# Stick-breaking logits from 64 array rows a head, in place of zero-padded queries of 128 rows

## The chip, the core and the metric

The kernel runs on one core of a Trainium2 chip. Its engines work side by side, each through its own queue in a fixed order: PE (TensorE) multiplies matrices into the eight PSUM banks, DVE (VectorE) and ACT (ScalarE) do elementwise work and read PSUM, POOL (GpSimd) does elementwise work on SBUF alone, SP (SyncE) starts most DMA transfers. Each waits only where its next instruction needs what another has not finished. The metric is the device time of one execution in microseconds (us), the median over runs.

## What is computed

One layer with 512 tokens and 16 meta tokens ahead of them, width 1024: two mixers side by side, an output projection with layer norm, and a mixture of 16 experts. The change concerns the second mixer, "stick breaking", with 8 heads of 64 columns:

```python
def stick_breaking_mixer(q, k, v, norm_g):
    qh = heads(q) * (SB_DH ** -0.5)
    kh, vh = heads(k), heads(v)
    for blk in range(Lp // Q_BLOCK):
        start = blk * Q_BLOCK
        end = start + Q_BLOCK
        z = jnp.einsum('bhqd,bhkd->bhqk', qh[:, :, start:end], kh[:, :, :end])
        mask = jnp.arange(end)[None, :] < (start + jnp.arange(Q_BLOCK))[:, None]
        log_keep = jnp.where(mask, jax.nn.log_sigmoid(-z), 0.0)
        log_a = jax.nn.log_sigmoid(z) + lax.cumsum(log_keep, axis=3, reverse=True) - log_keep
        a = jnp.where(mask, jnp.exp(log_a), 0.0)
        outs.append(jnp.einsum('bhqk,bhkd->bhqd', a, vh[:, :, :end]))
```

After both mixers, `layer_norm(ALPHA * h + mixed @ w_out)` is routed, and each token goes to two of the 16 experts.

## The kernel before

**Stages.** Until 243.5 us of the profiled execution PE makes the input projections (`projections`, L333), seven groups of 512 columns, each in three fp32r products of high and low parts (`mm3`, L126 to L130); the heads of the first mixer are woven in between. The last group is the stick-breaking queries. From 243.5 to about 365 us `stick_breaking` (L568) and `out_proj` (L815) are woven (L907). Then tokens are routed, and from about 392 us on the 16 experts run: their weights are split into a high part (ACT, L900) and a low part (DVE, L901) and multiplied.

**Queries and keys.** The projected keys of a pair of heads lie in one tile `skT[pr]` of 128 rows, 64 for each head. `ev_sq` (L386) evacuates a group's four products, each with the queries of one pair, into eight tiles `sqZ`: head 2c has its queries in rows 0 to 63 and zeros in the others, head 2c+1 the reverse. The zeros are POOL memsets (L393), the upper halves go through ACT (L395), the lower through DVE (L397). Two buffers of the pool `big` hold the eight tiles. A product of `sqZ[h]` with `skT[pr]` then runs over all 128 rows, of which 64 add nothing.

**A head.** `sb_weights` (L484) makes one head's logits in PSUM banks `pj` (there are four): for the last query block (528 keys) two banks of 264 columns, for the others one bank. A bf16 product with an identity (L493, L499) adds the mask. Then Abs (ACT, L504), a maximum with zero (DVE L508, for every fourth head ACT L506), Exp and Ln (ACT, L509, L510), a scan along the keys (DVE, L513), a subtraction of the scan from the logits (DVE, L515), which is the last reader of the bank, and a final Exp (ACT, L516). `sb_values` (L521) transposes the weights of a pair of heads (PE L529, copied by DVE L531) and multiplies them with the values (PE L536), one pair behind. `sb_finish` (L539) closes a block of queries. `UNITS` (L479) gives the order: the last query block with four pairs, then the third, then the first two together.

**The output projection.** `out_proj` first takes buffers of the pool `big` for two broadcast rows (loaded by ACT's queue, L236), for two raw weight tiles (`wo_half`, SP's queue, L716) and for their high and low parts (ACT L725, DVE or POOL L124 and L122). Per block of 128 tokens it runs 24 instructions of `mm3` into two `z` banks, and DVE adds the result to the residual (L832). The first half of the weights serves four blocks, the second half (L722, L723) comes later: 192 instructions in all.

**What sets the order.** A build step lists each engine's queue from the program's order, the dependences and when buffers of a pool come free; it is fixed before the run. The pool `big` has 14 buffers, and the pool `free` (L850) of seven takes the memory of `upool`, which is closed at L849 when the first mixer is done. The first seven expert loads go there (`pump`, L871), and each load waits until the third before it has landed (`DEPTH`).

Of the kernel before, what the change touches and what calls it, by code (L numbers as in the profile page):

```python
# [13 lines left out]
AF = mybir.ActivationFunctionType  # L14
OP = mybir.AluOpType
# [3 lines left out]
P = 128  # L19
# [62 lines left out]
def hymba_kernel(ctx: ExitStack, tc: tile.TileContext, x, meta, w_in, lbnd, hgg, sbg, w_out, ln1g, ln1b,  # L82
                 wrg, brg, wre, bre, wg, wu, wd, ln2g, ln2b, out):
    nc = tc.nc
    V = nc.vector
# [18 lines left out]
    pj = lambda shape=None: bank("pj", 4, shape)  # L104
# [86 lines left out]
    for i2 in range(2):  # L191
        xr_ = xr[i2]
        for i1 in range(2):
            i = 2 * i2 + i1
# [25 lines left out]
    for m in (16, 8, 4, 2, 1):  # L220
        t = upool.tile([P, P], I32, tag=f"lm{m}", bufs=1, name=f"lm{m}")
# [9 lines left out]
    identb = att.tile([P, P], BF, name="identb")  # L231
    maskb = att.tile([P, P], BF, name="maskb")
# [136 lines left out]
            yield 1  # L369


    skT, sqZ, svt = [], [], []
    vbd = att.tile([P, 512], F32, name="vbd")

    def ev_sk(c, acc):
# [8 lines left out]
            V.tensor_copy(skT[c][:, 0:NM], p_[:, c, :])  # L384

    def ev_sq(c, acc):  # L386
        if c % 2 == 0:
            t = big_tile(4)
            sqZ.extend(t[:, j] for j in range(4))
        for s in range(2):  # L390
            q_ = sqZ[2 * c + s]
            r, o = slice(64 * s, 64 * s + 64), slice(64 * (1 - s), 64 * (1 - s) + 64)
            nc.gpsimd.memset(q_[o], 0.0)  # L393
            if s:
                nc.scalar.activation(q_[r], acc[r], AF.Copy, scale=0.125)  # L395
            else:
                V.tensor_scalar(q_[r], acc[r], 0.125, None, op0=OP.mult)  # L397

    def ev_sv(i, acc):
        if i == 0:  # L400
# [80 lines left out]

    relu = [0]

    def sb_weights(pr, s, am, qts, spans, n):  # L484
        h = 2 * pr + s
        pieces = []
        if n == 528:
            for a in range(2):
                z = pj()
                nc.tensor.matmul(z[:, 0:264], sqZ[h][:, 384:512], skT[pr][:, 264 * a:264 * a + 264],  # L490
                                 start=True, stop=not a)
                pieces.append((z, 264 * a, 264))
            nc.tensor.matmul(z[:, 136:264], identb, maskb, start=False, stop=True)  # L493
        else:
            z = pj()
            for i, (a, b) in zip(qts, spans):
                nc.tensor.matmul(z[:, a:b], sqZ[h][:, i * P:(i + 1) * P], skT[pr][:, 0:b - a],
                                 start=True, stop=False)
                nc.tensor.matmul(z[:, b - P:b], identb, maskb, start=False, stop=True)  # L499
            pieces.append((z, 0, n))  # L500
        ll, cc = tt(), tt("zs", ZS_BUFS)
        relu[0] += RELU_SHARE
        for z, a, w in pieces:
            nc.scalar.activation(ll[:, a:a + w], z[:, 0:w], AF.Abs)  # L504
            if relu[0] // 8 != (relu[0] - RELU_SHARE) // 8:
                nc.scalar.activation(cc[:, a:a + w], z[:, 0:w], AF.Relu)  # L506
            else:
                V.tensor_scalar(cc[:, a:a + w], z[:, 0:w], 0.0, None, op0=OP.max)  # L508
        nc.scalar.activation(ll[:, 0:n], ll[:, 0:n], AF.Exp, scale=-1.0)  # L509
        nc.scalar.activation(ll[:, 0:n], ll[:, 0:n], AF.Ln, bias=1.0)  # L510
        for a, b in spans:
            rv = slice(b - 1, a - 1 if a else None, -1)
            V.tensor_tensor_scan(cc[:, rv], cc[:, rv], ll[:, rv], 0.0, op0=OP.add, op1=OP.add)  # L513
        for z, a, w in pieces:
            V.tensor_sub(cc[:, a:a + w], z[:, 0:w], cc[:, a:a + w])  # L515
        nc.scalar.activation(cc[:, 0:n], cc[:, 0:n], AF.Exp)  # L516
        for m, (a, b) in enumerate(spans):
            (nc.gpsimd if n != 416 else V).tensor_copy(am[:, m, h * NM:(h + 1) * NM], cc[:, a:a + NM])
        return cc
# [48 lines left out]
    def stick_breaking():  # L568
        todo = []
        st = {}  # L570

        def drain():
            pr, qts, spans, prs, am, bank_, zz = todo.pop(0)
            if pr == prs[0]:
                st["o"] = bank_()
            sb_values(prs.index(pr), pr, prs, st["o"], zz, qts, spans)
            if pr == prs[-1]:
                sb_finish(am, st["o"], prs, qts)

        for qts, spans, n, groups in UNITS:  # L580
            for g, prs in enumerate(groups):
                am = att.tile([P, 2, P], F32, tag="am", bufs=3, name="am")
                if len(prs) < 4:
                    nc.gpsimd.memset(am, 0.0)
                for m, pr in enumerate(prs):
                    zz = []
                    for s in range(2):
                        zz.append(sb_weights(pr, s, am, qts, spans, n))
                        yield 1
                    todo.append((pr, qts, spans, prs, am, pj if g == 1 else otb, zz))  # L590
                    if len(todo) > 1:
                        drain()
                        yield 1
        for i, bank_ in ((0, zb), (1, pj)):
            acc2[i] = [bank_(), bank_()]
            for n_ in range(EARLY):
                wo_mm(i, 4, wo2, acc2[i], (n_,))
        drain()
# [586 lines left out]
    for hf in range(2):  # L1185
# [9 lines left out]
        for k in range(4):  # L1195
            c = 4 * hf + k
# [223 lines left out]
```

## Time and profile before

| what | us |
|---|---|
| median of three runs (729.41 to 730.34) | 730.28 |
| profiled execution | 727.62 |
| its span, first to last instruction | 725.9 |
| PE busy in the span | 658.3 (91%) |
| DVE busy | 550.8 (76%) |
| ACT busy | 426.0 (59%) |
| POOL busy | 189.3 (26%) |
| heads of the last query block | 243.5 to 272 |
| heads of the other query blocks, output projection | 272 to 365 |
| experts | 392.5 to the end |

The busy times are sums over the span, and their shares are averages over stages with different limits. A matmul's row shows its latency, so consecutive rows overlap: how long PE needs for one is read from the distance of two starts.

### The profile page before, as it was taken

The page shows a single profiled execution, that of the slowest core. Times are in us where ns is not written, and L with a number is a line of the kernel's source. Part 1 is how long each engine was busy: PE and PEld are TensorE (multiplying, and loading weights), DVE is VectorE, ACT ScalarE, POOL GpSimd, SP SyncE. Part 2 cuts the span into 40 slices and gives each one's busy share as a digit, 9 for nine tenths or more (in the row PEclk, how much of TensorE's full clock was granted, in tenths as well). Part 3 has the DMA queues.
Part 4 walks back from the last instruction along what each step waited for, and adds up shares of the span by engine and source line. Part 5 has one row for each costly group of instructions (what it writes and reads, how often), then busy time and mean ns, then how long its engine had stood idle before and what let it go on. Part 6 is the DMA issues. An engine that isn't in the chain of part 4 may idle for free. (4 is left out here: it accounts for less than half of the span.)

```text
span 725.9 us, 9414 instructions
## 1 busy us (share of the span) xinstructions
PE 658.3 (91%) x3366; PEld 530.3 (73%) x3366; DVE 550.8 (76%) x851; ACT 426.0 (59%) x640; POOL 189.3 (26%) x187
## 2 busy tenths in 40 slices
PE   6999999999999999988775799999999999999870
PEld 5878878777877777777665688888778788787650
DVE  5333064655564896999678999999999999999885
ACT  5353243535262674946214588768688686798682
POOL 5101144333243100112352023413114132112213
PEclk9999999999999999999997899999999999999995
DMA  9341111030004870303552899999999999998612
GB/s 348 121 120 58 59 59 58 4 113 1 1 1 163 304 287 0 117 1 119 224 216 99 290 339 339 351 326 368 329 348 377 335 362 334 334 360 280 216 41 114
DMA packets 62307, 143.67 MB, mean 198 GB/s; under 512 B 7370, under 2 KB 7402, under 8 KB 62256
## 3 DMA queue, kind: packets, MB, share of 16 engines
q1 hardware_dynamic: 53600, 128.98, 49.2%
q0 software_dynamic: 5904, 12.82, 6.0%
q10 hardware_dynamic: 2752, 1.22, 0.8%
q8 instruction: 28, 0.46, 0.2%
q14 instruction: 23, 0.19, 0.1%
HBM read 137.01 MB, written 14.68 MB: 209 GB/s over the span
## 5 line engine op out<-in xcount | busy, mean ns | idle before, releaser
L901 DVE TENSOR_TENSOR b<-b 128x1024 fp32r<-128x1024 f32 x192 | 225.2, 1221 | 4.6 <-ACT b L900 4.6
L900 ACT ACTIVATE b<-b 128x1024 fp32r<-128x1024 f32 x192 | 189.5, 1054 | 14.9 <-PE pj L130 12.3
L128 PE MATMUL pj<-b 128*128 128x512 f32 x264 | 108.1, 412 | 3.4 <-ACTq L1088 2.6
L129 PE MATMUL pj<-b 128*128 128x512 f32 x264 | 106.5, 404 | 0.6 <-DVE b L124 0.6
L130 PE MATMUL pj<-b 128*128 128x512 f32 x264 | 106.3, 403 | 0.0
L129 PE MATMUL pj<-b,xl 128*128 128x512 f32 x224 | 87.7, 391 | 2.7 <-DVE xl L1200 2.7
L128 PE MATMUL pj<-b,xh 128*128 128x512 f32 x224 | 89.3, 400 | 0.2 <-ACT b L900 0.2
L130 PE MATMUL pj<-b,xh 128*128 128x512 f32 x224 | 86.3, 401 | 0.5 <-DVE b L901 0.5
L963 POOL DMA_INDIRECT xg<-h1d,idx x15 | 21.9, 1460 | 175.4 <-DVE gate L960 73.0
L128 PEld LDWEIGHTS pj<-b 128*128 128x128 f32 x264 | 50.6, 192 | 14.5 <-ACTq L1088 2.7
L124 DVE TENSOR_TENSOR b<-b 128x1024 fp32r<-128x1024 f32 x24 | 33.1, 1391 | 35.4 <-ACT b L329 31.9
L130 PEld LDWEIGHTS pj<-b 128*128 128x128 f32 x264 | 51.0, 193 | 11.2 <-issue 0.5
L129 PEld LDWEIGHTS pj<-b 128*128 128x128 f32 x264 | 51.1, 194 | 10.9 <-DVE b L124 0.9
L1010 POOL DMA_INDIRECT ad<-y,idx x14 | 46.7, 3334 | 39.8 <-ACT b L900 27.6
L129 PEld LDWEIGHTS pj<-b,xl 128*128 128x128 f32 x224 | 42.1, 188 | 11.6 <-DVE xl L1200 3.1
L130 PEld LDWEIGHTS pj<-b,xh 128*128 128x128 f32 x224 | 42.0, 188 | 11.2 <-DVE b L901 2.6
L329 ACT ACTIVATE b<-b 128x1024 fp32r<-128x1024 f32 x28 | 29.3, 1056 | 35.4 <-PE pj L130 15.2
L128 PEld LDWEIGHTS pj<-b,xh 128*128 128x128 f32 x224 | 42.1, 188 | 9.0 <-ACT b L900 1.5
L626 ACT ACTIVATE zs<-zs 128x512 f32<-128x512 f32 x28 | 17.7, 632 | 48.1 <-POOL zs L625 48.0
L122 POOL TENSOR_TENSOR b<-b 128x1024 fp32r<-128x1024 f32 x8 | 19.6, 2446 | 92.5 <-ACT b L329 73.0
L624 POOL TENSOR_TENSOR zs<-u 128x256 f32<-128x256 f32 x28 | 22.2, 793 | 63.7 <-issue 25.9
L513 DVE TENSOR_TENSOR_SCAN zs<-zs,t 128x528 f32<-128x528 f32 (+3 forms) x32 | 32.8, 1046 | 2.0 <-ACT t L510 1.9
(339 smaller groups left out, 1325.3 us busy)
## 6 DMA issues: line engine op xcount, KB each, us to landing
b<-in_w_exp_gate_dram SPq DMA_DIRECT2D x32, 1024.0 KB, 8.3
b<-in_w_exp_up_dram SPq DMA_DIRECT2D x32, 1024.0 KB, 8.3
b<-in_w_exp_down_dram SPq DMA_DIRECT2D x32, 1024.0 KB, 10.0
b<-in_w_in_dram SPq DMA_DIRECT2D x12, 1024.0 KB, 5.0
b<-in_x_dram SPq DMA_DIRECT2D x8, 512.0 KB, 8.0
b<-in_w_out_dram SPq DMA_DIRECT2D x4, 1024.0 KB
b<-in_w_in_dram SPq DMA_DIRECT2D x4, 512.0 KB
h1d<-b POOLq DMA_DIRECT2D x4, 512.0 KB, 2.9
```

Source lines behind the costliest of these rows:

```text
L122: nc.gpsimd.tensor_sub(dst, src, hi)
L124: V.tensor_sub(dst, src, hi)
L128: nc.tensor.matmul(acc, ah, bh, start=first, stop=False)
L129: nc.tensor.matmul(acc, al, bh, start=False, stop=False)
L130: nc.tensor.matmul(acc, ah, bl, start=False, stop=last)
L329: latest[0] = nc.scalar.activation(wt[:, 0], src, AF.Copy).ins
L513: V.tensor_tensor_scan(cc[:, rv], cc[:, rv], ll[:, rv], 0.0, op0=OP.add, op1=OP.add)
L624: nc.gpsimd.tensor_sub(xv[:, :, 0, :], ref, bv[:, :, 0, :])
L900: nc.scalar.activation(t[:, 0], raw, AF.Copy)
L901: V.tensor_sub(t[:, 1], raw, f32(t[:, 0]))
L963: nc.gpsimd.indirect_dma_start(out=dst, out_offset=None, in_=h1d, in_offset=bass.IndirectOffsetOnAxis(ap=idx, axis=0), bounds_check=T - 1, ...
L1010: nc.gpsimd.indirect_dma_start(out=ad, out_offset=bass.IndirectOffsetOnAxis(ap=idx, axis=0), in_=y, in_offset=None, bounds_check=T - 1, oo ...
```

## The change

`ev_sq` writes one tile `sqT[c]` of 128 rows a pair, as the keys have it, with one ACT instruction; the memsets and the DVE half are gone, and one buffer of `big` is used where there were two. A new function `sb_logits` makes the products of both heads of a pair: operands are rows 0 to 63 for the first head and 64 to 127 for the second, one behind the other, and the masks of both follow. `sb_weights` gets the finished banks.

```diff
     def ev_sq(c, acc):
-        if c % 2 == 0:
+        if c == 0:
             t = big_tile(4)
-            sqZ.extend(t[:, j] for j in range(4))
-        for s in range(2):
-            q_ = sqZ[2 * c + s]
-            r, o = slice(64 * s, 64 * s + 64), slice(64 * (1 - s), 64 * (1 - s) + 64)
-            nc.gpsimd.memset(q_[o], 0.0)
-            if s:
-                nc.scalar.activation(q_[r], acc[r], AF.Copy, scale=0.125)
-            else:
-                V.tensor_scalar(q_[r], acc[r], 0.125, None, op0=OP.mult)
+            sqT.extend(t[:, j] for j in range(4))
+        nc.scalar.activation(sqT[c], acc, AF.Copy, scale=0.125)
...
-    def sb_weights(pr, s, am, qts, spans, n):
-        h = 2 * pr + s
-        pieces = []
+    def sb_logits(pr, qts, spans, n):
+
+        pieces = [], []
+        rows = [slice(64 * s, 64 * s + 64) for s in range(2)]
         if n == 528:
             for a in range(2):
-                z = pj()
-                nc.tensor.matmul(z[:, 0:264], sqZ[h][:, 384:512], skT[pr][:, 264 * a:264 * a + 264],
-                                 start=True, stop=not a)
-                pieces.append((z, 264 * a, 264))
-            nc.tensor.matmul(z[:, 136:264], identb, maskb, start=False, stop=True)
+                z = [pj(), pj()]
+                for s, r in enumerate(rows):
+                    nc.tensor.matmul(z[s][:, 0:264], sqT[pr][r, 384:512], skT[pr][r, 264 * a:264 * a + 264],
+                                     start=True, stop=not a)
+                    pieces[s].append((z[s], 264 * a, 264))
+            for s in range(2):
+                nc.tensor.matmul(z[s][:, 136:264], identb, maskb, start=False, stop=True)
         else:
-            z = pj()
+            z = [pj(), pj()]
             for i, (a, b) in zip(qts, spans):
-                nc.tensor.matmul(z[:, a:b], sqZ[h][:, i * P:(i + 1) * P], skT[pr][:, 0:b - a],
-                                 start=True, stop=False)
-                nc.tensor.matmul(z[:, b - P:b], identb, maskb, start=False, stop=True)
-            pieces.append((z, 0, n))
+                for s, r in enumerate(rows):
+                    nc.tensor.matmul(z[s][:, a:b], sqT[pr][r, i * P:(i + 1) * P], skT[pr][r, 0:b - a],
+                                     start=True, stop=False)
+                for s in range(2):
+                    nc.tensor.matmul(z[s][:, b - P:b], identb, maskb, start=False, stop=True)
+            for s in range(2):
+                pieces[s].append((z[s], 0, n))
+        return pieces
+
+    def sb_weights(pr, s, pieces, am, qts, spans, n):
+        h = 2 * pr + s
...
+                    pieces = sb_logits(pr, qts, spans, n)
                     for s in range(2):
-                        zz.append(sb_weights(pr, s, am, qts, spans, n))
+                        zz.append(sb_weights(pr, s, pieces[s], am, qts, spans, n))
```

The queues change in more places than the diff. SP's queue after the last loads for the input projections, before (`in_w_out` are the output projection's weights, `in_w_exp` the experts'):

```order
L179 DMA b<-in_w_in_dram 128x4x512 x12
L716 DMA b<-in_w_out_dram 128x2x1024 x2
L877 DMA b<-in_w_exp_gate_dram 128x4x512
L877 DMA b<-in_w_exp_up_dram 128x4x512
L877 DMA b<-in_w_exp_gate_dram 128x4x512
```

and in the changed kernel:

```order
L881 DMA b<-in_w_exp_gate_dram 128x4x512
L881 DMA b<-in_w_exp_up_dram 128x4x512
L881 DMA b<-in_w_exp_gate_dram 128x4x512
L720 DMA b<-in_w_out_dram 128x2x1024 x2
L828 DMA b<-in_x_dram 128x1024 x4
```

The two weight loads of the output projection have moved behind all seven of the first expert loads (the last three of them are shown).

ACT's queue from the end of the first mixer to the first heads, before (`b<-b 128x1024` at L725 are the splits of the output projection's weights, `b<-pj` the queries' evacuation, `t<-pj` the Abs):

```order
L469 ACTIVATE t<-oT 128x512
L725 ACTIVATE b<-b 128x1024
L472 ACTIVATE t<-z,eps_rms 128x512
L725 ACTIVATE b<-b 128x1024
L473 ACTIVATE t<-t 128x512
L463 ACTIVATE b<-t 128x512
L725 ACTIVATE b<-b 128x1024 x2
L395 ACTIVATE b<-pj 64x512 x2
L504 ACTIVATE t<-pj 128x264
L395 ACTIVATE b<-pj 64x512 x2
```

and in the changed kernel, where the same splits (now L729) stand, at the third and fourth pair of the last query block:

```order
L729 ACTIVATE b<-b 128x1024 x2
L519 ACTIVATE zs<-zs 128x528
L507 ACTIVATE t<-pj 128x264 x2
L512 ACTIVATE t<-t 128x528
L509 ACTIVATE zs<-pj 128x264
L513 ACTIVATE t<-t 128x528
L507 ACTIVATE t<-pj 128x264
L509 ACTIVATE zs<-pj 128x264
L512 ACTIVATE t<-t 128x528
L513 ACTIVATE t<-t 128x528
L729 ACTIVATE b<-b 128x1024 x2
L519 ACTIVATE zs<-zs 128x528 x2
```

The splits stood before the first head and now stand inside the work of the last pairs.

PE's queue at the second pair of the last query block, before (`tr<-ident,zs` are the transposes of the first pair's weights, `z<-b` the output projection):

```order
L490 MATMUL pj<-skT,b 128x264 x2
L493 LDWEIGHTS identb
L493 MATMUL pj<-maskb,identb 128x128
L529 MATMUL tr<-ident,zs 128x128 x4
L490 MATMUL pj<-skT,b 128x264 x2
L493 LDWEIGHTS identb
L493 MATMUL pj<-maskb,identb 128x128
L129 MATMUL z<-b 128x512
```

and in the changed kernel:

```order
L485 MATMUL pj<-skT,b 128x264 x2
L532 MATMUL tr<-ident,zs 128x128 x4
L485 MATMUL pj<-skT,b 128x264 x2
L489 LDWEIGHTS identb
L489 MATMUL pj<-maskb,identb 128x128
L489 LDWEIGHTS identb
L489 MATMUL pj<-maskb,identb 128x128
L532 MATMUL tr<-ident,zs 128x128 x4
L539 MATMUL oT<-b,aT 128x64 x8
```

The first two products were both halves of one head's keys; now they are the first half of both heads, and the second halves of both come after the transposes. No output-projection instruction stands between. PE's queue now has none of them until the fourth pair's products, where before it had 25 up to there.

## Rows read from the trace of the kernel before

**Rows 1.** Stretch, busy us of PE, PEld, DVE, ACT, POOL (instructions); clock, DMA share, GB/s.
```profile
243.50:272.00 28.50, 26.63 (x151) 20.94 (x150) 25.41 (x46) 21.49 (x47) 2.08 (x8) 1.00 0.85 331
272.00:288.50 16.50, 16.06 (x84) 11.87 (x83) 9.96 (x17) 6.02 (x13) 1.17 (x5) 1.00 0.00 0
288.50:307.00 18.50, 18.03 (x102) 13.81 (x101) 16.76 (x26) 16.95 (x33) 3.22 (x6) 1.00 0.35 115
...
392.50:726.00 333.50, 299.15 (x1413) 237.86 (x1412) 308.18 (x404) 246.10 (x304) 79.79 (x36) 0.96 0.85 297
```
**Rows 2.** Timeline of PE (start us, us, engine, line): products of queries and keys, mask.
```profile
250.04 1.16 PE L490 MATMUL pj<-skT,b 128*128 128x264 f32 x4 [0.26 <-DVE zs L515]
251.03 0.22 PE L493 MATMUL pj<-maskb,identb 128*128 128x128 bf16 x1
...
288.25 0.84 PE L497 MATMUL pj<-skT,b 128*128 128x400 f32 x2
288.92 0.22 PE L499 MATMUL pj<-maskb,identb 128*128 128x128 bf16 x1
```
**Rows 3.** Timeline of PE around a 16-row product, then two full ones.
```profile
228.38 0.39 PE L130 MATMUL pj<-b 128*128 128x512 f32 x1
228.70 0.48 PE L674 MATMUL tr<-u,t 16*128 16x128 f32 x2
229.11 0.94 PE L676 MATMUL tr<-b,t 128*128 128x128 f32 x6
...
231.02 0.39 PE L686 MATMUL oT<-qd,t 128*128 128x128 f32 x2
231.25 0.39 PE L685 MATMUL oT<-aT,b 128*128 128x128 f32 x2
```
**Rows 4.** Timeline of ACT and DVE around the queries' evacuation; in brackets idle before.
```profile
233.40 1.06 ACT L725 ACTIVATE b<-b 128x1024 fp32r<-128x1024 f32 x1 [0.40 <-DMA b<-in_w_out_dram]
...
240.28 1.23 DVE L124 TENSOR_TENSOR b<-b 128x1024 fp32r<-128x1024 f32 x1 [0.26 <-ACT b L725]
241.74 2.72 DVE L397 TENSOR_SCALAR b<-pj 64x512 f32<-64x512 f32 x4 [0.23 <-PE pj L130]
...
245.09 1.08 ACT L395 ACTIVATE b<-pj 64x512 f32<-64x512 f32 x2
```
**Rows 5.** Groups of ACT, 240 to 306: count | busy us, mean ns | idle before.
```profile
L504 ACT ACTIVATE t<-pj 128x264 f32<-128x264 f32 x16 | 5.9, 384 | 1.0 <-PE pj L490 0.9
L509 ACT ACTIVATE t<-t 128x528 f32<-128x528 f32 x8 | 5.2, 649 | 0.1
```
**Rows 6.** Timeline of DVE: first scan; second, fourth and eighth head's subtractions.
```profile
248.26 1.26 DVE L513 TENSOR_TENSOR_SCAN zs<-zs,t 128x528 f32<-128x528 f32 x1
...
251.52 0.77 DVE L515 TENSOR_TENSOR zs<-pj,zs 128x264 f32<-128x264 f32 x2
...
258.42 0.76 DVE L515 TENSOR_TENSOR zs<-pj,zs 128x264 f32<-128x264 f32 x2
...
271.15 0.77 DVE L515 TENSOR_TENSOR zs<-pj,zs 128x264 f32<-128x264 f32 x2
```
**Rows 7.** Timeline of POOL, the first three of eight memsets.
```profile
215.36 1.64 POOL L393 MEMSET b<- 64x512 f32 x3
```
**Rows 8.** Timeline of SP's DMA queue: start us, us, line, issue.
```profile
228.58 3.90 SPq L716 DMA_DIRECT2D b<-in_w_out_dram  x2
238.77 0.37 SPq L877 DMA_DIRECT2D b<-in_w_exp_gate_dram  x1
...
249.42 0.37 SPq L877 DMA_DIRECT2D b<-in_w_exp_up_dram  x1
252.03 0.37 SPq L877 DMA_DIRECT2D b<-in_w_exp_gate_dram  x1
```
**Rows 9.** Timeline of PE after waits, at the lower clock.
```profile
355.27 0.63 PE L129 MATMUL pj<-b 128*128 128x512 f32 x1
355.70 0.63 PE L130 MATMUL pj<-b 128*128 128x512 f32 x1
```

More of the change, by code (lines that the diff above doesn't have):

```diff
@@ L369, in projections @@
             yield 1
-    skT, sqZ, svt = [], [], []
+    skT, sqT, svt = [], [], []
     vbd = att.tile([P, 512], F32, name="vbd")
```

## Prediction

> **What bounds the kernel now.** I read the page's totals first, then the busy times by stretch, then the timeline of each queue from 215 to 310 us. The profiled execution takes 727.62 us, of which the span is 725.9; the median of the three runs is 730.28, so 2.66 us more. PE is busy 91% of the span, as the table above has it, but that is an average over stages. From 392.5 us on the experts run, and PE (299.15) and DVE (308.18) fill the 333.5 us between them [rows 1]. The change touches nothing there, and the stage starts when routing is known, so whatever the attention stage gains or loses before it should reach the end one for one. What decides is 243.5 to 365 us, where the stick-breaking heads and the output projection share the engines. With the eight heads of the last query block (243.5 to 272) DVE is busy 25.41 of 28.5 us. Then, from 272 to 288.5, PE is full (16.06 of 16.5) while DVE has only 9.96 us of work: PE catches up with the output projection. From 288.5 to 307 both are nearly full. So DVE with its chain through ACT sets the first stretch, and PE the second.
>
> **The products themselves.** A head's product against keys has two instructions for each 264 columns. Two such products and the mask's turn take 250.04 to 251.03, so about 0.5 us a product, and one of 400 columns takes 288.25 to 288.92, 0.67 us [rows 2]. Sixteen of the first, eight of the second and eight pairs of 144 and 272 columns (an estimate of 0.7 each, by columns) make 19 us. The operand now has 64 rows, but the columns streamed are as many, so PE gains only where the two heads of a pair run beside each other. No row of this trace shows two 64-row products, so the bounds are: nothing saved, or half, 9.5 us. The nearest row for other row counts is the 16-row product: the instruction before it starts at 228.38, it starts at 228.70 and the next full one at 229.11. Two such instructions took 0.50 us of PE's time where two full ones take 0.22 to 0.23 [rows 3], so a visit to another shape costs about 0.28 us. There are 20 visits in the new order (7 in the first query block, 5 in the second, 8 in the last): up to 5.6 us lost. I take neither end: half of the products' gain on 64 rows given back by visits, and no net saving on the path. [...]
>
> **The evacuation of the queries.** Before, DVE does four halves (241.74 to 244.46) and ACT four, the last ending at 246.17 [rows 4]. After, ACT does four full tiles at about 0.57 us, each as its product ends, so until 244.4. Then its order is three Abs of 0.38 (pipelined, 0.3 apart), an Exp of 0.65, an Abs and an Ln [rows 5], and the first scan can start at about 247.2 instead of 248.26 [rows 6]: 1.1 us gained. But ACT's new order puts the final Exp of the pair's first head ahead of the Ln of the second head. That Exp waits for scan and subtractions (1.26 and 0.7) until 249.1, Exp and Ln take it to 250.4, and with the second scan, one maximum and the subtractions [rows 6] the pair ends at 252.8, where before its last subtractions ran from 251.52 to 252.3. The gain is spent: +0.5 us.
>
> **Two heads at once in four banks.** With 528 columns a pair fills all four pj banks. Before, the next head's two banks were free as soon as one head's subtractions were done. Now the second halves of both heads of the next pair need the banks of both heads before. So after a pair's last subtraction there is a chain that DVE fills only in part: two products and masks (until about +0.7 us), two Abs, Exp, maximum on ACT, Ln (to +3.1), scan, subtractions, scan, subtractions (3.9): 7.0 to 7.1 us a pair without overlap, 6.6 with it. Before, the subtractions starting at 258.42 and 271.15 lie two pairs apart [rows 6], 6.4 us a pair. Pairs two and three cost +0.6 each: the third ends at about 266.9, +1.6 us in all.
>
> **The weights that come late.** This is what the change moves without saying so. The eight POOL memsets of 0.5 us from 215.36 on [rows 7] had no input, so, as I read the order, they claimed the query tiles' buffers early, and the output-projection weights, next in line for buffers of the same pool, could be loaded at 228.58 [rows 8] and split on ACT from 233.40 [rows 4]. Now the first writer of the query tile is ACT's evacuation at 241.7. In the new order the two weight loads stand behind seven expert loads on SP's queue. Those start at 238.77, are each held until the third before has landed, and by 249.42 and 252.03 advance 2.6 us a piece [rows 8]; four are still to land at 252. The broadcast rows that ACT loads now share the time. So the first weights land at about 262 to 265, the second 2.6 us later, and the 25 output-projection instructions that PE did ahead of the fourth pair cannot run there. Nothing else fills PE's gaps. ACT reaches the first two splits at about 267, so it hardly waits for the data, but the splits, 1.05 us each, now lie in its chain: two ahead of the third pair's last Exp and the fourth pair's Abs, two ahead of the fourth pair's final Exps. Three of the low parts (1.23 us each [rows 4]) lie in DVE's chain, one of them between the last scan and its subtractions. The fourth pair's first scan is then due at 271.9, its last subtraction ends at about 277.7; before, it ended at 271.9: **+5.8 us**. Then PE takes over: its queue up to the next pair holds 70 output-projection instructions less the first 12, at 0.23 us, the transposes and values between, and the second pair of the next query block starts its product at about 295.0, before at 288.25 [rows 2]: **+6.8**. Up to that point 76 of the 192 output-projection instructions were done before, 70 are now, so no more is left over than 6 times 0.23 us.
>
> **What is given back.** From 288.5 to 307 PE was nearly full, and the six heads that are left there have products of 4 us: up to 2 us saved with overlap, nothing without. DVE's idle 1.7 us there bounds the recovery. I take 0.8 us. The memsets that go and the 2.7 us of DVE that go were hidden: POOL and DVE both waited around them, with PE full ahead of 243.5. **Sum: 6.8 less 0.8, +6.0 us**, so 733.6 for an execution like the profiled one and 736.3 for the median. Bounds: with full overlap the three chains give back 0.45 each, the block's pair 0.67 and the block after some 1.2 more, +3; without overlap and with the price of each visit on the path (7 before 277, 5 in the next block, 3.4 us) and PE falling to its lower clock after a wait of some 5 us, as the 0.43 us from 355.27 to 355.70 shows (0.23 otherwise) [rows 9], +11.
>
> **Rivals.** (1) *The pairs do not run beside each other and the shape changes cost*: the change then does not do what it says, and gives the upper bound. For it speaks the 16-row product [rows 3], against it that a 64-row pair may lie in two halves of the array at once. [...] Time: 730.3 + 10, about 740. (2) *Faster*: PE is the bound of 272 to 307, and a pair side by side saves there 8 times 0.33 us, 2.7 us, while the first scan starts 1.1 us earlier. This decides if the late weights cost nothing, that is if they land by about 258, before the third pair's end, and their splits find ACT idle (it was busy 21.49 of 28.5 us [rows 1]). Time: about 727.5. Against it: seven loads at 2.6 us stand in front. (3) *No change*: the 25 instructions moved (5.8 us) are paid by 64-row pairs (4 us up to 288.5) and by the gaps that PE has later, since from 307 on DVE sets the pace: 730 to 731.5. Against it: DVE was idle 6.5 us from 272 to 288.5 because PE was late, and will be again.
>
> **How the numbers follow.** Forecast 62% (733.5 to 738.5), rival 1 17%, rival 2 10%, rival 3 11%. The time is the forecast's, 736.3. The range leaves out the faster rival, half of the no-change one and the far end of rival 1: 730.5 to 742. Within 0.2% is 728.8 to 731.7, about what measurement can tell from no change. Faster 0.10, same 0.11, slower 0.79.
>
> **What will show it.** The weight loads issued after about 250 us on SP instead of 228.58; ACT's first split after 262; no output-projection product before the fourth pair; the last subtraction of the 528-column heads near 277; PE full between there and the next block's second pair at about 295; the expert stage as long as before, 333.5 us. Starts of the two products of a pair within some 0.1 us of each other would show overlap; 0.25 apart per instruction, none. Wrong would be: weights landed before 258, subtractions two pairs apart still 12.8 us, or an expert stage that shortens.

## The result, and the profile after

The changed kernel takes 740.45 us (median of 4 runs, 738.66 to 741.25), the kernel before beside it 729.85: a ratio of 1.0141, 95% interval [1.0112, 1.0170], so 10.6 us slower. The forecast was 736.3, with a range of 730.5 to 742. The direction and the range hold, the size was too small, and the time that came is almost the one that rival 1 gave, for a cause that was not rival 1's. The profiled execution took 741.25 us, with a span of 739.5.

The page's totals and clock row (40 slices, tenths of full speed):

```profile
span 739.5 us, 9413 instructions
PE 666.1 (90%) x3366; PEld 533.2 (72%) x3366; DVE 548.9 (74%) x847; ACT 424.6 (57%) x640; POOL 176.4 (24%) x179
...
PEclk9999999999999669999997999999999999999895
```

The same stretches as in [rows 1], from the first product of queries and keys on (columns as there):

```profile
243.40:278.70 35.30, 30.62 (x136) 23.11 (x136) 27.40 (x45) 23.79 (x49) 3.98 (x7) 0.66 0.87 334
278.70:297.00 18.30, 17.17 (x89) 13.04 (x87) 10.05 (x18) 5.39 (x12) 2.80 (x7) 1.00 0.01 1
297.00:403.80 106.80, 85.67 (x539) 68.88 (x538) 89.10 (x195) 48.07 (x103) 28.89 (x25) 0.92 0.35 129
403.80:739.50 335.70, 300.37 (x1412) 238.92 (x1412) 307.86 (x403) 245.92 (x304) 71.16 (x36) 0.95 0.85 295
```

The heads of the last query block take 35.3 us instead of 28.5, and PE's granted clock in them is 0.66 instead of 1.00. SP's queue shows why (start, us, line, issue):

```profile
249.21 0.37 SPq L881 DMA_DIRECT2D b<-in_w_exp_up_dram  x1
253.26 0.37 SPq L881 DMA_DIRECT2D b<-in_w_exp_gate_dram  x1
253.68 1.01 SPq L720 DMA_DIRECT2D b<-in_w_out_dram  x2
```

And ACT's timeline has the splits of these weights:

```profile
268.63 2.00 ACT L729 ACTIVATE b<-b 128x1024 fp32r<-128x1024 f32 x2
...
274.76 1.99 ACT L729 ACTIVATE b<-b 128x1024 fp32r<-128x1024 f32 x2
```

The first load of the output projection's weights is issued at 253.68, before at 228.58 [rows 8], and they are split at 268.63 and 274.76, before from 233.40 on [rows 4]. DVE's timeline shows the ends of the four pairs (the last subtraction of each) and the low parts, L124:

```profile
251.59 0.76 DVE L518 TENSOR_TENSOR zs<-pj,zs 128x264 f32<-128x264 f32 x2
...
259.27 0.77 DVE L518 TENSOR_TENSOR zs<-pj,zs 128x264 f32<-128x264 f32 x2
...
266.54 1.42 DVE L518 TENSOR_TENSOR zs<-pj,zs 128x264 f32<-128x264 f32 x4
...
269.71 2.36 DVE L124 TENSOR_TENSOR b<-b 128x1024 fp32r<-128x1024 f32 x2 [0.44 <-ACT b L729]
...
276.85 1.20 DVE L124 TENSOR_TENSOR b<-b 128x1024 fp32r<-128x1024 f32 x1
...
277.96 0.77 DVE L518 TENSOR_TENSOR zs<-pj,zs 128x264 f32<-128x264 f32 x2
```

And PE's timeline, at the second pair, the first output-projection product, a wait for a low part, the next block's second pair, and a wait of the last block of queries:

```profile
248.56 1.65 PE L485 MATMUL pj<-skT,b 64*128 64x264 f32 x4 [3.06 <-DVE zs L518]
...
270.15 0.78 PE L128 MATMUL z<-b 128*128 128x512 f32 x1
...
280.33 0.50 PE L130 MATMUL z<-b 128*128 128x512 f32 x1 [1.04 <-POOL b L122]
...
297.01 0.94 PE L494 MATMUL pj<-skT,b 64*128 64x400 f32 x4
297.88 0.28 PE L497 MATMUL pj<-maskb,identb 128*128 128x128 bf16 x2
...
339.31 0.55 PE L532 MATMUL tr<-ident,zs 128*128 128x128 f32 x3 [2.96 <-ACT zs L519]
339.61 0.62 PE L130 MATMUL z<-b 128*128 128x512 f32 x1
340.04 0.63 PE L128 MATMUL z<-b 128*128 128x512 f32 x1
```

A pair of 400 columns takes 0.87 us (297.01 to 297.88) where one padded head took 0.67 [rows 2]: the pairs do run beside each other. But the second pair of that block starts 8.8 us later than before (297.01 against 288.25).

### The profile page after: what moved, and what is told of

The parts are those of the page before. It is cut to its first block, busy times and chain, and to the rows that moved or that the text cites. A ratio compares the mean times of both kernels' runs of the same rounds, so it can differ in the third digit from the quotient of the medians.

```text
span 739.5 us, 9413 instructions
## 1 busy us (share of the span) xinstructions
PE 666.1 (90%) x3366; PEld 533.2 (72%) x3366; DVE 548.9 (74%) x847; ACT 424.6 (57%) x640; POOL 176.4 (24%) x179
## 5 line engine op out<-in xcount | busy, mean ns | idle before, releaser
L130 PE MATMUL pj<-b 128*128 128x512 f32 x264 | 106.2, 402 | 0.0
L967 POOL DMA_INDIRECT xg<-h1d,idx x15 | 20.2, 1348 | 182.6 <-DVE gate L964 75.6
L124 DVE TENSOR_TENSOR b<-b 128x1024 fp32r<-128x1024 f32 x24 | 33.0, 1389 | 32.3 <-ACT b L329 31.8
L1014 POOL DMA_INDIRECT ad<-y,idx x14 | 39.5, 2825 | 42.9 <-DMA b<-in_w_exp_gate_dram 18.3
L516 DVE TENSOR_TENSOR_SCAN zs<-zs,t 128x528 f32<-128x528 f32 (+3 forms) x32 | 29.3, 942 | 4.2 <-ACT t L513 4.0
```

Source lines behind the costliest of these rows:

```text
L124: V.tensor_sub(dst, src, hi)
L130: nc.tensor.matmul(acc, ah, bl, start=False, stop=last)
L967: nc.gpsimd.indirect_dma_start(out=dst, out_offset=None, in_=h1d, in_offset=bass.IndirectOffsetOnAxis(ap=idx, axis=0), bounds_check=T - 1, ...
L1014: nc.gpsimd.indirect_dma_start(out=ad, out_offset=bass.IndirectOffsetOnAxis(ap=idx, axis=0), in_=y, in_offset=None, bounds_check=T - 1, oo ...
```

## The experiments

The first column of this table is the start of the first product; the others are counted from it in each profiled execution, because the projections ahead end up to 3 us apart. "Block" is the end of the last subtraction of the 528-column heads, "second 400" the start of the second pair of 400 columns, "experts" the first expert product. Medians and ratios are over all runs; the kernel before had medians of 729.3 to 730.5 beside them.

| kernel | first product, us | block | second 400 | experts | median us | ratio to before |
|---|---|---|---|---|---|---|
| before | 244.03 | 27.9 | 44.2 | 148.5 | 729.3 | |
| changed | 243.39 | 35.3 | 53.6 | 160.4 | 740.45 | 1.0141 |
| e1_early | 243.46 | 30.8 | 42.7 | 148.9 | 728.59 | 0.9992 |
| e2_late | 244.71 | 28.8 | 50.0 | 158.8 | 738.9 | 1.012 |
| e3_headwise | 244.35 | 31.2 | 44.7 | 154.5 | 734.89 | 1.0066 |
| e4_same_rows | 245.76 | 33.9 | 46.3 | 155.0 | 731.91 | 1.0029 |
| e5_filler | 243.88 | 41.2 | 57.9 | 165.1 | 745.72 | 1.0207 |
| e6_padded_last | 242.68 | 27.9 | 46.2 | 155.2 | 733.87 | 1.0051 |
| e7_416_headwise | 245.52 | 30.8 | 42.7 | 152.6 | 732.93 | 1.0036 |
| e8_clock | 244.94 | 35.9 | 52.9 | 162.7 | 741.69 | 1.0162 |
| e9_mid | 243.71 | 37.6 | 54.8 | 163.6 | 741.59 | 1.016 |
| e10_pool_low | 243.56 | 30.8 | 42.7 | 149.4 | 728.45 | 0.9982 |
| e11_no_low | 243.59 | 35.7 | 55.9 | 163.7 | 743.54 | 1.0183 |

### Weights early or late

The changed kernel with an early claim of the query tile:

```diff
             sqT.extend(t[:, j] for j in range(4))
+            nc.gpsimd.memset(t[:, :, 0:8], 0.0)
```

> The changed kernel, but one small POOL memset writes a strip of the query tile early, as the removed memsets did; the output projection's weight loads then stand ahead of the expert loads again. Late-weights theory (the weights, and the lower PE clock that follows because nothing fills PE's gaps, are most of the 10.6 us): weight loads near 229 us, granted clock 1.0 from 243 to 272, the 528-column heads end near 273 to 274 instead of 278.7, time 728 to 734. Rival (64-row products cost more than 128-row ones, by shape changes): the time stays at 738 to 741 with early weights.

The ratio is 0.9992 [0.9974, 1.001]. The two weight loads are issued at 219.24 and 227.84, and the clock is whole in the heads of the last query block (busy times by stretch, columns as in [rows 1]):

```profile
243.40:274.20 30.80, 29.73 (x174) 22.63 (x174) 25.75 (x47) 20.58 (x47) 1.83 (x7) 1.00 0.81 307
```

That one strip takes the whole loss away. The 64-row products are in this kernel as in the changed one, so rival 1 falls. The other side is the kernel before with nothing but late loads:

```diff
-            nc.sync.dma_start(raw, rap(w_out, ...))
+            d_ = nc.sync.dma_start(raw, rap(w_out, ...))
+            if not base:
+                tc.add_manual_dep(d_.ins, loads[R_FREE - 1].name, ... NoSync ...)
```

> The kernel before with its 128-row padded products, and the two weight loads of the output projection ordered behind the seven expert loads on SP, nothing else. Late-weights theory: 737 to 741 (7 to 11 us slower), clock near 0.66 from 248 to 271, the 528-column heads end near 276 to 279. Rival (the 64-row products are the cost): 730 to 732, the weights' loads are hidden.

The ratio is 1.012 [1.0093, 1.0147], 9.6 us: padded products and late weights cost nearly what the change costs. The expectation was wrong about the place: the block ends only 0.9 us later than before (28.8 against 27.9), and the clock is 0.94 in it, not 0.66. The loss appears behind it. PE's timeline in this kernel, in the block and at the next one's second pair:

```profile
250.43 1.16 PE L490 MATMUL pj<-skT,b 128*128 128x264 f32 x4 [3.03 <-DVE zs L515]
...
276.08 0.50 PE L128 MATMUL z<-b 128*128 128x512 f32 x1 [1.48 <-ACT b L728]
...
280.55 0.73 PE L130 MATMUL z<-b 128*128 128x512 f32 x2 [1.35 <-DVE b L124]
...
294.68 0.84 PE L497 MATMUL pj<-skT,b 128*128 128x400 f32 x2
```

PE waits in the block with nothing to fill it, then for splits, and then has the output projection to catch up with.

### The products alone

Early weights, 64-row products, but head after head (the loops of the kernel before with `sqT[pr][r, ...]` and `skT[pr][r, ...]`):

> Products of 64 rows, but one head after the other as in the kernel before (no pair shares the array, two banks a head), and the early strip, so weights are early. If the order of two heads in four banks costs 0.6 us a pair (my step), the 528-column heads end 1 to 2 us earlier than with the pairs. If running the two row groups beside each other is worth more (0.4 us a pair of 400 columns), this one is 1 to 3 us slower than the paired kernel with early weights. By the shape-change rival, it is slowest: 730.3 plus 40 visits at 0.28 us, up to 741.

Ratio 1.0066 [1.004, 1.0093], 6.3 us above e1_early. The block is no shorter than with pairs (31.2 against 30.8), but PE is full in it (31.55 of 32.0 us), so what the order of two heads in four banks costs can't be read here; e6_padded_last, below, has 27.9. Without a partner beside it, a 64-row product makes for a slower kernel, but the 5.6 us over the kernel before are not all its price. The first product of 144 columns starts 78.4 us after the first of all, before 76.6, with the clock whole up to there. The 4.2 us lost behind that, up to the third pair of those blocks (25.0 us against 20.8), fall where the first head's scans took 5.17 us beside POOL's work and the granted clock was 0.86. Then the pair with both heads in the same rows:

```diff
-        rows = [slice(64 * s, 64 * s + 64) for s in range(2)]
+        rows = [slice(0, 64) for s in range(2)]
```

> The paired kernel with early weights, but both heads of a pair use rows 0 to 63 (the second head's logits are then those of the first: part of the computation is changed). Same order of instructions, no two row groups. If the row groups run beside each other: a pair of 400 columns takes 1.3 to 1.5 us instead of 0.87, and the time is 1 to 4 us above the paired kernel with early weights. If they don't: 0.87 us as before, no difference.

Ratio 1.0029 [1.0011, 1.0046], 3.3 us above e1_early: the pairs' overlap is real. (The profiled execution was the slowest of its ten, 736.25 us, so its row in the table ends later than the median would.) The same products, up to the mask, on PE's timeline; first e1_early, with two row groups:

```profile
286.16 0.94 PE L495 MATMUL pj<-skT,b 64*128 64x400 f32 x4
287.03 0.28 PE L498 MATMUL pj<-maskb,identb 128*128 128x128 bf16 x2
```

Then e4_same_rows, with one:

```profile
292.05 1.61 PE L495 MATMUL pj<-skT,b 64*128 64x400 f32 x4
293.59 0.28 PE L498 MATMUL pj<-maskb,identb 128*128 128x128 bf16 x2
```

And e3_headwise, a head alone:

```profile
289.00 0.94 PE L492 MATMUL pj<-skT,b 64*128 64x400 f32 x2
289.87 0.23 PE L494 MATMUL pj<-maskb,identb 128*128 128x128 bf16 x1
```

A pair takes 0.87 us beside each other and 1.54 one behind the other. A head alone takes 0.87 where the padded product took 0.67 [rows 2]: the 64 rows cost 0.20 us a visit and save nothing by themselves. Removing the zeros alone makes the products dearer; the overlap pays it back.

### The lower clock

Needless products at PE's waits, in the changed kernel with its late weights, behind the Ln of a head:

```diff
         nc.scalar.activation(ll[:, 0:n], ll[:, 0:n], AF.Ln, bias=1.0)
+        if n == 528 and h < 3:
+            if h == 0:
+                fill.append(zb())
+            for _ in range(2):
+                nc.tensor.matmul(fill[0][:, 0:264], ident, ll[:, 0:264], start=True, stop=True)
```

The first form of it had them for six heads (`h < 6`):

> The changed kernel with its late weights, and two needless products of 264 columns (about 0.5 us each, into a bank that nobody reads) behind each Ln of the first six heads of the last query block: PE has something to do while it waits for scan and subtractions. If the lower clock after PE's waits is part of the loss: granted clock above 0.9 instead of 0.66 from 243 to 279, 7.0 to 7.2 us a pair instead of 7.7 to 7.9, last subtraction of the 528-column heads near 277 instead of 278.7, time 736 to 739. If the chain through ACT and DVE hides PE's clock: pairs as long as before, 740 to 742.

Ratio 1.0207 [1.0178, 1.0236]. Six heads' fillers moved other instructions as well: the fourth pair's second products went behind the output projection, to 272.71. Its first three pairs say what was asked, 7.1 us each, but its time says nothing. The second form leaves every other row in its place:

> The changed kernel with its late weights and every other row of every queue in its place; two needless products of 264 columns (about 0.5 us each) behind the Ln of the first three heads alone, at PE's waits. If the lower clock lengthens the chain: from the first pair to the third about 7.1 us a pair instead of 7.7 and 7.9, the third pair's last subtraction ends near 266.5 instead of 267.96, the fourth's 1 to 1.5 us earlier too, time 738 to 739.5 against 740.45. If it does not: pairs as long as before, 740 to 741.

Ratio 1.0162 [1.0137, 1.0188], no better than the changed kernel. DVE's ends of the four pairs:

```profile
253.15 0.76 DVE L524 TENSOR_TENSOR zs<-pj,zs 128x264 f32<-128x264 f32 x2
...
260.24 0.77 DVE L524 TENSOR_TENSOR zs<-pj,zs 128x264 f32<-128x264 f32 x2
...
266.60 1.43 DVE L524 TENSOR_TENSOR zs<-pj,zs 128x264 f32<-128x264 f32 x4
...
276.84 3.32 DVE L124 TENSOR_TENSOR b<-b 128x1024 fp32r<-128x1024 f32 x1
280.09 0.76 DVE L524 TENSOR_TENSOR zs<-pj,zs 128x264 f32<-128x264 f32 x2
```

PE's granted clock was 0.93 from 244.9 to 268.0, where the changed kernel had 0.59 from 243.4 to 268.0, and the pairs end at 253.91, 261.01 and 268.03, 7.1 and 7.0 us apart, instead of 7.7 and 7.9. So the lower clock does lengthen the chain, by 1.5 us up to the third pair. In the fourth it is gone: a low part of 1.2 us takes 3.32 there, beside POOL's own, which began 0.4 us before it (the last section). That the clock lengthens the chain is shown; that it reaches the end is not. The second pair of 400 columns starts 0.7 us sooner than in the changed kernel (52.9 against 53.6), but the stretch from there to the first product of 144 columns takes 35.5 us at a granted clock of 0.90, where the changed kernel took 33.0 at 1.00.

### What in the late weights costs

The loads in the middle: seven expert loads become three, then the weights between the others:

```diff
-    pump(R_FREE)
+    pump(3)
     weave(stick_breaking(), out_proj(), WO_RATIO)
...
         wo = wo_half(0)
+        pump(R_FREE - 3)
```

> The changed kernel with the first of the two weight loads of the output projection behind three expert loads on SP instead of seven, the second behind two more; nothing else is edited. They should land near 250 and 258 and their splits stand at the second and the third pair. If the loss comes from PE's work that cannot run while the weights are missing, it falls with the lateness: 733 to 737, between the early (728.6) and the late kernel (740.45). If loads that land by 258 cost nothing, as my rival of a faster kernel had it: 728 to 731. If the splits inside the chain are the cost, wherever they stand: 738 to 741.

Ratio 1.016 [1.0132, 1.0188]: as slow as with all seven ahead. ACT's first split waits for the data of the first load, which so landed before 258:

```profile
253.29 1.06 ACT L729 ACTIVATE b<-b 128x1024 fp32r<-128x1024 f32 x1 [1.13 <-DMA b<-in_w_out_dram]
```

DVE's ends of the first three pairs show where the time goes:

```profile
251.92 0.76 DVE L518 TENSOR_TENSOR zs<-pj,zs 128x264 f32<-128x264 f32 x2
...
262.28 0.77 DVE L518 TENSOR_TENSOR zs<-pj,zs 128x264 f32<-128x264 f32 x2
...
272.77 0.77 DVE L518 TENSOR_TENSOR zs<-pj,zs 128x264 f32<-128x264 f32 x2
```

The second and third pair take 10.4 and 10.5 us, each with two splits (2.0 to 2.1 us on ACT) and their low parts in its chain: two on DVE (2.5 us) in the second, one on DVE and one on POOL in the third, beside which a scan of 1.25 us took 3.10. PE now has 30 output-projection products more in hand at the first pair of 400 columns than in the changed kernel (42 against 12), and still nothing is won, because the chain is longer by as much. Lateness and loss do not go together: with the first split 15 us earlier the loss is the same. What the rows suggest is that it counts whether the splits stand ahead of the heads or among them; no run moved the splits alone, and in e2_late splits among the last heads lengthened the block by only 0.9. The condition of my rival 2 was loads that land by 258 and splits that find ACT idle; the rows show the first load in time, and its splits in the chain all the same.

Then the changed kernel without the low parts, in which `wo` gets the high part twice:

```diff
-                    lo_sub(t[:, 1], raw[:, k, :], f32(t[:, 0]), WO_SHARE)
-                wo.append((t[:, 0], t[:, 1]))
+                wo.append((t[:, 0], t[:, 1 if base else 0]))
```

> The changed kernel with its late weights and ACT's splits where they are, but the low parts of the first half of the output projection's weights are left out (the high parts are used twice, as many products as before; part of the computation is changed): the three low parts of 1.2 us in DVE's chain and POOL's one go. If the chain through DVE at the fourth pair decides what reaches the end: last subtraction 3 to 3.7 us earlier (near 275), time 736 to 738. If PE's missing work decides (25 output-projection products that could not run while the weights were missing, at 0.23 us): the block ends earlier, but the second pair of 400 columns starts within 1 us of 297 and the time is 739.5 to 740.5.

Ratio 1.0183 [1.0166, 1.0201]: both expectations missed, it is slower than the changed kernel. Without the low parts PE's products stand elsewhere in its queue, and ACT waits 0.95 us for PE's transposes ahead of the fourth pair's maximum; the block ends at 35.7 instead of 35.3, and the second pair of 400 columns starts at 55.9, with PE full from 277.7 on. Since the order on PE changed with them, the run does not tell what DVE's low parts cost by themselves. How the loss divides between PE's backlog and the splits in the chain stays open.

### Attempts at a better version

Three more with early weights. With padded queries for the last block alone (one tile of 128-column queries with zeros, products head after head, as before):

> Early weights; the last query block with padded queries head after head, as in the kernel before (zeros and halves of 128 queries alone), the other blocks with pairs of 64-row products. If two heads at once in four banks cost 2.3 us in that block (274.2 against 271.9 for the last subtraction) and it reaches the end: block ends at 272 or earlier, time 725.5 to 727.5. If what is gained there is given back where DVE sets the pace from 296 to 318: 728 to 729.

Ratio 1.0051 [1.0033, 1.007]. The block is as short as before (27.9), 2.9 us less than in e1_early, and the experts start 6.3 us later than there. Shortening the first chain gave nothing here: the gain is gone by the second pair of 400 columns (46.2 against 42.7), and in the 20 us from 311 on the granted clock was 0.83. What else in the queues takes it back is open.

With the two 416-column query blocks head after head:

> The paired kernel with early weights, but in the first two query blocks (416 columns) each head's 64-row products and masks come one head after the other, so that the first head's scan can start ahead of two long POOL operations. If the pair's order costs there 1 to 2 us (DVE's scans of both heads fall into POOL's 4.8 us): second scan ends about 1 us after POOL instead of 2.2, time 727 to 728. If not, the shape visits make it 0 to 1 us slower: 728.6 to 730.

Ratio 1.0036 [1.0001, 1.007], 4.3 us above e1_early. The aim was missed: the first head's scans start at 325.92, 0.24 us behind POOL's first operation (325.68), and take 5.14 us. The granted clock fell in that stretch, too (a product of 272 columns took 1.27 us instead of 0.72), so what the order alone costs, or a scan ahead of POOL would gain, is not told by this run.

With one low part of the second half on POOL:

> The paired kernel with early weights, and one of the four low parts of the second half of the output projection's weights made on POOL (two operations) instead of DVE, which is busy 21.5 of the 22.5 us from 296 to 318.5. If DVE sets the pace there: 1 to 2 us less, 726.5 to 727.5, the best of all. If POOL's long operations slow DVE's scans beside them (3.2 and 4.3 us where a scan pair otherwise takes 1.06): no gain or a loss, 728.6 to 731.

Ratio 0.9982 [0.9963, 1.0001], the lowest median of all, and by its interval no different from before and from e1_early. PE waited 1.34 us for POOL's part at 306.59, and the first product of 144 columns starts 2.2 us later than in e1_early (34.5 against 32.3 us behind the second pair of 400 columns). The stretch after it is 2.3 us shorter, which bears on the step that failed, below.

## Why the prediction was right or wrong

**The products: no net saving. Right in the time, in part by luck.** e1_early has all of the new products and is at 0.9992. The price of a visit was put at 0.28 us from a 16-row product [rows 3] and is 0.20 on 64 rows. The overlap is whole: 0.67 us saved on a pair of 400 columns (1.54 less 0.87), of which a visit gives back 0.20, where the sum had half. So PE did gain, about 0.47 us on such a pair, and e1_early is 1.5 us ahead of the kernel before at the second of them. It is the stretch behind it that takes the gain back, which the sum had not. No row of before could show the overlap, so the half was an estimate of mine; e1_early against e4_same_rows shows it.

**The evacuation: +0.5.** The first pair ended at 252.35 where 252.8 was forecast. Counted from the first product it took 9.0 us, before 8.3. Right.

**Two heads in four banks: 7.0 to 7.1 us a pair.** Right at a granted clock of 0.93 with no output-projection products between (e8_clock: 7.1 and 7.0). In e1_early, at 1.00 with output-projection products between, the ends of the pairs lie 8.0, 7.0 and 8.0 us apart, and the block is 2.9 us longer than before, where the sum had 2.3. In the changed kernel, at 0.59 up to 268.0, it was 7.7 and 7.9, since the sum took PE's clock as whole, and named the lower one only in the upper bound, after "a wait of some 5 us". No row shows that wait: those of [rows 9] stand behind waits of 1.76 and 2.56 us, and in the changed kernel the clock was down after one of 3.06. The third pair ended at 267.96, forecast 266.9: 1.1 us of the miss.

**The weights that come late: right in place, short in size.** Loads behind seven expert loads, splits in the third and fourth pair, no output-projection product until 270.15, a last subtraction at 278.73 (forecast 277.7), and 70 output-projection instructions ahead of the next block's second pair, as counted. That pair started at 297.01, forecast 295.0. The 2.0 us that are missing match the 1.1 of the clock and a wait of 1.04 us for POOL's low part at 280.33, which the sum had not. e1_early and e2_late show the cause: with the loads early the changed kernel loses nothing, with them late the kernel before loses 9.6 us. The reason behind the size was only half seen. The sum put the loss on the chain of the fourth pair and 6 products. In e2_late the chain is hardly longer and the loss comes from PE; in e9_mid PE's work is back in its gaps and the chain is longer by as much.

**What is given back: the step that failed.** The sum had 0.8 us returned between the second pair and the experts. That stretch is 106.8 us (297.0 to 403.8) against 104.25 before (288.25 to 392.5): 2.5 us lost where 0.8 were to come back, so 3.3 of the 5.3 us by which the profiled executions (11.3 us apart at the first expert product) miss the sum of 6.0. It isn't the late weights: e1_early has 106.2 there too. Of the 2.5 us, 1.4 lie in one place. From the first product of 144 columns to that of the third pair it was 20.8 us before:

```profile
320.60 0.41 PE L497 MATMUL pj<-skT,b 128*128 128x144 f32 x2
...
341.39 0.41 PE L497 MATMUL pj<-skT,b 128*128 128x144 f32 x2
```

In the changed kernel it is 22.2, as in e1_early:

```profile
329.96 0.52 PE L494 MATMUL pj<-skT,b 64*128 64x144 f32 x4
...
352.14 0.52 PE L494 MATMUL pj<-skT,b 64*128 64x144 f32 x4
```

PE waits there for the first head's Exp, 2.96 us at 339.31, and its next eight products start 0.43 us apart instead of 0.23, 1.6 us, at a granted clock of 0.50 from 340 to 342. Before, it waited less, and the granted clock was 1.00 from 327 to 333:

```profile
328.44 0.55 PE L529 MATMUL tr<-ident,zs 128*128 128x128 f32 x3 [1.31 <-ACT zs L516]
...
331.11 0.43 PE L536 MATMUL oT<-b,aT 128*128 128x64 f32 x2 [1.19 <-DVE aT L531]
```

The Exp waits for DVE, and DVE's scans stand beside two long operations of POOL. DVE's first scans and POOL's first operation, before:

```profile
323.65 3.23 DVE L513 TENSOR_TENSOR_SCAN zs<-zs,t 128x144 f32<-128x144 f32 x2
...
323.83 2.46 POOL L762 TENSOR_TENSOR b<-b 128x1024 f32<-128x1024 f32 x1 [7.57 <-ACT t L510]
```

And in the changed kernel:

```profile
332.56 2.37 POOL L766 TENSOR_TENSOR b<-b 128x1024 f32<-128x1024 f32 x1 [7.02 <-ACT t L507]
...
333.79 4.20 DVE L516 TENSOR_TENSOR_SCAN zs<-zs,t 128x144 f32<-128x144 f32 x2 [0.91 <-ACT t L513]
...
335.01 2.40 POOL L767 TENSOR_TENSOR b<-b 128x1024 f32<-128x1024 f32 x1
```

The two scans of a head took 1.06 us with no POOL operation beside them (341.14). Before, they began 0.18 us ahead of POOL's first operation. Now that the logits of both heads come first, that operation is 1.23 us ahead of them. In e10_pool_low they took 2.44 us, PE waited 1.20, and the same stretch is 19.9 us. That agrees, but other rows moved in that kernel as well, and no run moved the scan alone. As I read it, the overlap's saving on PE was of no use here, since from 307 to 354 DVE is the busier engine (before, from 307 to 320.6: 12.85 of 13.6 us, PE 11.41). The other 1.1 of the 2.5 us are open.

**The end.** 8.8 and 2.5 make 11.3 us at the first expert product. The expert stage was to stay at 333.5 us; it took 335.7, and 335.7 in e1_early too, which lost nothing over its runs, so I count it as the spread of executions, which is not shown. The median says 10.6.

**The rivals.** Rival 1 gave 740, and 740.45 came: had there been only the time, it would have seemed right. Its half about the price of 64 rows is true in kind (0.20 us a visit, and e3_headwise is slower than before), its other half, no overlap, is false, and together they cost nothing in e1_early. Rival 2's mechanism was in e1_early, which reaches the second pair of 400 columns 1.5 us sooner than before (42.7 against 44.2), but its gain went on the way to the experts (148.9 against 148.5). Rival 3's payment by later gaps did not come about.

## What to carry to other kernels

When a change removes instructions, ask what these claimed, not only what they took: here memsets without an input held a place in a pool's order, and with them went the loads of another stage and 10 us. Then look whether the thing that comes late also carries work for the engines in the critical chain, for here it cost as much in the middle of the chain as at its end. And put a time that agrees to the test like one that doesn't: the number of a wrong rival can come out.

## What the runs showed of the hardware

**DVE and POOL beside each other.** In e8_clock POOL's low part began 0.4 us ahead of DVE's, in the changed kernel the two began together. POOL's timeline of e8_clock:

```profile
276.44 2.65 POOL L122 TENSOR_TENSOR b<-b 128x1024 fp32r<-128x1024 f32 x1 [4.68 <-ACT b L735]
```

And in the changed kernel:

```profile
276.82 3.45 POOL L122 TENSOR_TENSOR b<-b 128x1024 fp32r<-128x1024 f32 x1 [4.70 <-ACT b L729]
```

In e8_clock DVE's instruction of 1.2 us took 3.32 (from 276.84) and ended 1.07 us after POOL's. In the changed kernel DVE took its 1.20 (from 276.85) and POOL 3.45, where the same split took 2.43 in the kernel before (241.34) and 2.50 in e3_headwise (237.69), both beside other DVE instructions. So in both cases one engine took about its usual time, and the other longer by about as much as the first still had to run: in e8_clock DVE by 2.1 us, where POOL had 2.25 left, in the changed kernel POOL by about 1.0 us beside DVE's 1.20. In e8_clock the one that began first ran through. In the changed kernel the starts are 0.03 us apart, and the profile's times for POOL are rough, so which was first is not told. The changed kernel's scans at 333.79, beside POOL's operations of 2.37 and 2.40 us, took 4.20 us instead of 1.06. A list of busy times doesn't show it, since all of the 3.32 or 4.20 us count as busy.

**The clock.** In the changed kernel PE's granted clock was 1.00 from 243.40 to 245.40. PE waited 3.06 us behind the mask at 245.27, and the products at 248.56 then took 1.58 us for four instructions, where six had taken 1.08 at 243.39. The granted clock was 0.50 from there to 270.15; then output-projection products followed each other, and from 272.37 on they start 0.23 us apart, where the first two were 0.57 apart. In e2_late a wait of 3.03 us was followed by four instructions that took 0.99 us up to the mask, as in the kernel before [rows 2], and only the four from 252.49 on took 1.89: the length of the one wait alone does not tell.
